# A two-layer decoder step: tables in the source fix the order of four engines' queues, and the first norm sums into two single banks

## The chip, the cores and the metric

The kernel runs on one core of a Trainium2 chip. The time is the device time of one execution in microseconds (us); three runs of the kernel before gave 983.78 (the median), 988.02 and 983.61 us.

In what follows, PE is the engine for matrix products (PEld its loading of the stationary operand), DVE the vector engine, ACT the engine for activation functions, POOL the general-purpose one, and SP the engine whose queue issues the transfers (DMAs). Each works through a queue of its own in order; an instruction that has to wait for another engine holds up what stands behind it in its queue.

## The reference

One step of a decoder trunk with two layers, for a prompt of 512 tokens and for 8 samples of 4 new tokens each, with D = 1024 and 16 heads of 64. Every layer computes, in float32,

```
x <- x + W_out( mixer(RMSNorm(x)) * silu(z) )        # z: a gate path out of the layer's input projection
layer 0: mixer = RWKV-7   # token shift, low-rank decay and gates, then per head
                          #   S_t = S_(t-1) (diag(w_t) - kk_t (a_t kk_t)^T) + v_t k_t^T ;  o_t = S_t r_t
layer 1: mixer = NSA      # 16 query heads, 4 KV heads, three branches that are gated and summed:
                          #   attention over compressed blocks (32 rows, stride 16),
                          #   over the 16 best blocks of 64 rows, and over a window of 512 rows
```

The results are the new x, the recurrence's states, the shift rows and the K/V rows of both groups.

## The kernel before

**Layout.** The 544 tokens stand as columns in two halves of 272 (256 of the prompt, 16 of the samples); features are on the partitions. Each float32 operand is split into a high and a low part (line L300 writes the high part on ACT, L301 the rest on POOL or DVE), and `products` (L339) takes three products for each block of 128 features: high x high, high x low, low x high. Such a matmul has the form 128*128 128x272; it goes to the sums `ph` or `pp` in PSUM. PE's stream is mostly these. They are also the filler around everything that waits.

**Layer 0.** First the norm (`rstd`: squares on ACT in pairs, `L418` sums them over the partitions with a matrix of ones, `L420` takes the logarithm, `L421` the exponential), then the projections, then the recurrence in chunks: a triangular inversion by 32 small steps (`L1139` multiply and `L1140` reduce, on DVE, for all heads at once, with tiles `tmp` and `i`), transposes (`L1167`), small products of 64x64 and 32x32 on PE (`L1171`, `L1180`, `L1190`, `L1333`, `L1340`, `L1354`, and from then on `L1237` to `L1292` chunk by chunk) with a mask or a sum on DVE behind each (`L1173`, `L1181`, `L1336`, `L1345`, `L1346`, `L1356`, `L1243`, `L1245`, `L1259`), and the samples' own recurrence (`L1311`, `L1378`, `L1379`, `L1385`, `L1394`, `L1397`, `L1402`). The gates' products run beside them as filler, and so does the first part of the output projection.

**Layer 1.** The input projection again by L339 into `ph`, scaled by the norm's row on DVE (`L1594`), the query and key norms (`L1601`, `L1608`, `L1610`, `L1613`); the attention for the prompt in blocks of 128 queries, `L1855` scores into `pq`, `L1882` bias, mask and row maximum (DVE), `L1889` the exponential (ACT), `L1894` to `L1909` the normalising (DVE, on ACT as `L1907`), `L1933` transposes of the weights into another `pq`, `L1936` (ACT) and `L1938` (DVE) copies of these out of PSUM, `L1946` and `L1949` products with the values into `pw`. The compressed branch has weights `cc`, transposed at `L1921`. The samples' attention (`L2007`, `L2014`, `L2029`, `L2050`, `L2084`) lies between; the gate products `L1643` to `L1656` stand at the start of the layer. The output projection is L339 and `L2127` with `L2141` adding the residual, and its last part `L2209` with `L2210`. The two `pq` tiles, one `pw` and three `ph` are all that layer 1 has in PSUM: whoever wants the next `pq` waits until one has been read.

**What sets the order.** The kernel is traced once in Python; the generators in it say which pieces follow each other, and then the library's scheduler sets the order of each engine's queue, by its own estimate of durations:

```
    with tile.TileContext(nc, schedule_with_timeline_sim=True) as tc, ExitStack() as ctx:
        build(nc, tc, ctx, I, O)
```

So the order in the queues isn't the one in the source, and no line of the source names it.

Of the kernel before, what the change touches and what calls it, by code (L numbers as in the profile page):

```python
# [228 lines left out]
class K:  # L229
# [175 lines left out]

    def rstd(self, X):
        nc = self.nc
        pt = self.PP()
# [1879 lines left out]
```

## Time and profile before

| | |
|---|---|
| times of three runs | 983.61, 983.78, 988.02 us |
| the profiled execution | 991.15 us, span 989.4 us, mean granted clock of PE 0.975 |
| busy | PE 937.0 us (95%), DVE 661.6 (67%), ACT 565.0 (57%), POOL 396.1 (40%) |
| the chain that ended last | PE 51%, DVE 14%, DMA 6%, ACT 5%, issue 5%, POOL 2% |
| transfers | 157.47 MB, 159 GB/s mean |

A profile is one execution; its rows show when each instruction started, for how long it ran, and what released it when its engine had been idle. The profiled execution took 7.4 us more than the median of the three runs (0.75%), so durations out of it are set against its own 991.15 us first.

A row of the timeline gives start and duration in us, engine, line, operation, the tile written and the tiles read, the form, how many instructions the row groups, and in brackets the engine's idle time ahead of it in us with its releaser. A row of the waits gives a waiting line, what it waited for, the total in us, how often, and the longest. A row of the table by stretches gives for each engine busy us and instructions, and after POOL the granted clock of PE (1.00 is full speed), the busy share of the transfer engines and GB/s.

### The profile page before, as it was taken

How to read it: one execution, taken by the hardware profiler on the slowest of the kernel's cores; microseconds unless marked ns; L12 is line 12 of the kernel's file. 1: busy time of each engine (PE TensorE's matmuls, PEld its weight loads, DVE VectorE, ACT ScalarE, POOL GpSimd, SP SyncE). 2: the span in 40 equal slices, each digit the busy share in tenths (PEclk: the TensorE clock that was granted, in tenths of full speed). 3: DMA queues.
4: the chain of work that ended last, by engine and by line, in shares of the span. 5: the costliest groups of instructions: out<-in, count | busy, mean ns of one | idle time of the engine just before them, and what ended most of it. 6: DMA issues, size and time to landing. Idle time of an engine off the chain costs nothing.

```text
span 989.4 us, 24773 instructions
## 1 busy us (share of the span) xinstructions
PE 937.0 (95%) x9445; PEld 843.5 (85%) x9445; DVE 661.6 (67%) x1533; ACT 565.0 (57%) x1369; POOL 396.1 (40%) x480
## 2 busy tenths in 40 slices
PE   8899999999799998999999999999898999999997
PEld 7889998889787787887888889998787898887987
DVE  6987778897847442456867734846877466748755
ACT  5455786565262345535645646756767675857542
POOL 4416645453320544230313576554344253341430
PEclk9999999999897997999989999999999999999999
DMA  5686236569383344564564596432634433476634
GB/s 193 183 268 210 65 118 204 166 197 281 104 231 92 124 141 139 162 200 101 168 194 129 190 280 226 142 99 75 161 95 121 118 99 124 116 188 211 199 117 136
DMA packets 149240, 157.47 MB, mean 159 GB/s; under 512 B 52226, under 2 KB 97058, under 8 KB 148866
## 3 DMA queue, kind: packets, MB, share of 16 engines
q1 hardware_dynamic: 149122, 155.90, 52.3%
q8 instruction: 74, 1.21, 0.5%
q14 instruction: 44, 0.36, 0.1%
HBM read 112.25 MB, written 43.80 MB: 158 GB/s over the span
## 4 chain that ended last, share of the span: by engine, by line
PE 51%; DVE 14%; DMA 6%; ACT 5%; issue 5%; POOL 2%; SPq 2%; DVEq 0%; POOLq 0%; ACTq 0%
PE ph L339 24%; PE pq L1855 3%; PE pw L1946 3%; PE pq L1933 3%; PE pr L1237 2%; DVE tmp L1139 1%; ACT l L300 1%; PE ph L2209 1%; PE ph L384 1%; POOL l L301 1%; PE s L1271 1%; DVE a L1909 1%; DMA d<-dram 1%; ACT a L1889 1%; DVE l L301 1%
## 5 line engine op out<-in xcount | busy, mean ns | idle before, releaser
L339 PE MATMUL ph<-x,l 128*128 128x272 f32 x2412 | 349.3, 296 | 4.5 <-DVE l L301 1.6
L339 PEld LDWEIGHTS ph<-x,l 128*128 128x128 f32 x2412 | 318.9, 192 | 18.9 <-issue 7.1
L301 POOL TENSOR_TENSOR l<-w,l 128x512 fp32r<-128x512 f32 (+2 forms) x118 | 157.0, 1341 | 157.6 <-ACT l L300 146.8
L300 ACT ACTIVATE l<-w 128x512 fp32r<-128x512 f32 (+2 forms) x152 | 88.9, 612 | 102.5 <-PE ph L339 47.9
L339 PE MATMUL pp<-x,l 128*128 128x272 f32 x768 | 107.1, 293 | 1.7 <-DVE bs L682 1.7
L339 PEld LDWEIGHTS pp<-x,l 128*128 128x128 f32 x768 | 100.0, 188 | 3.8 <-issue 2.6
L1889 ACT ACTIVATE a<-a,st 128x512 f32<-128x512 f32 (+3 forms) x128 | 70.6, 553 | 23.2 <-DVE st L1882 22.8
L1855 PE MATMUL pq<-p,z 128*128 128x512 f32 (+7 forms) x288 | 58.5, 328 | 6.8 <-DVE st L1882 4.2
L1882 DVE CUSTOM_DVE_ANT_0 a<-pq,tb 128x512 f32<-128x512 f32 (+3 forms) x128 | 56.7, 485 | 8.8 <-PE pq L1855 8.6
L1855 PEld LDWEIGHTS pq<-p,z 128*128 128x128 f32 x288 | 42.7, 189 | 12.7 <-issue 4.4
L339 PE MATMUL pp<-t,l 128*128 128x272 f32 x384 | 53.0, 291 | 0.0
L1909 DVE TENSOR_SCALAR a<-a,st 128x128 f32<-128x128 f32 (+3 forms) x112 | 50.7, 507 | 0.7
L339 PEld LDWEIGHTS pp<-t,l 128*128 128x128 f32 x384 | 49.9, 188 | 0.5
L1933 PE MATMUL pq<-cst,a 128*128 128x128 f32 x320 | 48.9, 275 | 1.0 <-DVE a L1909 0.9
L1594 DVE TENSOR_TENSOR d<-ph,RS 128x272 f32<-128x272 f32 x56 | 24.3, 437 | 32.7 <-PE ph L339 32.0
L1933 PEld LDWEIGHTS pq<-cst,a 128*128 128x128 f32 x320 | 37.1, 140 | 4.8 <-issue 2.2
L1946 PE MATMUL pw<-h,p 128*64 128x256 f32 x320 | 38.1, 384 | 2.2 <-DVE h L1938 1.5
L1936 ACT ACTIVATE h<-pq 128x512 f32<-128x512 f32 x52 | 30.2, 592 | 16.5 <-PE pq L1933 16.3
L301 POOL TENSOR_TENSOR d<-d,d 128x544 fp32r<-128x544 f32 (+2 forms) x19 | 25.5, 1344 | 32.5 <-ACT d L300 32.4
L301 DVE TENSOR_TENSOR l<-w,l 128x512 fp32r<-128x512 f32 x34 | 32.6, 967 | 8.8 <-ACT l L300 4.4
L1237 PE MATMUL pr<-ab,ab 64*64 64x128 f32 x256 | 33.6, 281 | 1.3 <-ACT q L1223 0.7
L1946 PEld LDWEIGHTS pw<-h,p 128*64 128x64 f32 x320 | 21.6, 136 | 14.7 <-DVE h L1938 2.3
(454 smaller groups left out, 1937.7 us busy)
## 6 DMA issues: line engine op xcount, KB each, us to landing
w<-in_rkvz SPq DMA_DIRECT2D x64, 256.0 KB, 4.3
d<-dram SPq DMA_DIRECT2D x60, 272.0 KB, 3.6
w<-in_win SPq DMA_DIRECT2D x56, 256.0 KB, 3.0
dram<-d SPq DMA_DIRECT2D x48, 272.0 KB, 2.8
ab<-dram SPq DMA_DIRECT2D x32, 256.0 KB, 4.1
p<-in_xT SPq DMA_DIRECT2D x16, 272.0 KB, 5.2
tb<-dram SPq DMA_DIRECT2D x16, 264.0 KB, 7.6
dram<-uar SPq DMA_DIRECT2D x8, 512.0 KB
```

What stands on the lines that cost most here:

```text
L300: nc.scalar.activation(hi, raw, AF.Copy)
L301: (eng or nc.gpsimd).tensor_tensor(lo, raw, hi.bitcast(F32), OP.subtract)
L339: nc.tensor.matmul((pt[h][:m, :HN] if split else pt[:m, h, :HN]), a[:, k, :m], b[:, h * HN:(h + 1) * HN], start=(k == 0 and n == 0), stop= ...
L1237: nc.tensor.matmul(pg[par][r, i], BK[r, i, par], AR[r, i].rearrange("p a b -> p (a b)"), start=True, stop=True)
L1594: self.nc.vector.tensor_tensor(o, p, r, OP.mult)
L1855: nc.tensor.matmul(p[:, par], QZ[k, b][x][:, par, m], kk[:, lo:hi], start=(x == 0), stop=(x == 1))
L1882: nc.vector.tensor_tensor_reduce(out=P[par][j], in0=p[:, par, :n], in1=TB[k][:, g, o:o + n], scale=-1.0, scalar=3.0e38, op0=OP.add, op1=OP ...
L1889: nc.scalar.activation(P[par][j], P[par][j], AF.Exp, scale=-1.0, bias=st[:, 0, g, j + 1:j + 2], accum_out=st[:, 1, g, j + 1:j + 2])
L1909: (nc.gpsimd if e == "p" else nc.vector).tensor_scalar(pj, pj, rr, None, op0=OP.mult)
L1933: nc.tensor.transpose(pt[:, g % 2, g // 2], PB[g][j][:, c * 128:c * 128 + 128], ident)
L1936: nc.scalar.activation(w, pt, AF.Copy)
L1946: nc.tensor.matmul(po[r], v, W[x][:, par], start=(x == ns - 1), stop=False, skip_group_check=True)
```

## The change

Two things. First, four lists of numbers for layer 0's recurrence (`TURNS`) and four for layer 1 (`TURNS1`), one each for PE, DVE, ACT and POOL. `mark` notes how many instructions an engine has been given at that point; `queue` cuts what it has been given since into groups, at the numbers of its list, puts the groups into the list's order, and binds each instruction to the one ahead of it, without a semaphore, so that the scheduler has to keep that order. SP has no list. Second, `rstd` sums into two tiles of one bank each (`s0`, `s1`, a bank for each half of the columns) instead of the two-bank `pp`, and so takes the logarithm in two instructions, one for each half. The next users of `s0` and `s1`, the low-rank rows' products at L448, now come behind these reads.

```
+TURNS = {
+    "PE": [48, 0, 24, 19, 28, 22, 36, 64, 82, 73, ...
...
+TURNS1 = {
+    "PE": [0, 16, 41, 11, 27, 43, 13, 29, 45, 15, ...
...
     def rstd(self, X):
-        pt = self.PP()
+        pt = [self.t(tag, (128, 512)) for tag in ("s0", "s1")]
...
-        self.keep_busy(pt[:, 0, 0:128], 16, made, ones, ones)
+        self.keep_busy(pt[0][:, 0:128], 16, made, ones, ones)
...
-                self.squared = nc.tensor.matmul(pt[:, h, :HN], ones, ...
+                self.squared = nc.tensor.matmul(pt[h][:, :HN], ones, ...
...
-        nc.scalar.activation(self.h2(rs), pt[:, :, :HN], AF.Ln, bias=self.C("eps"))
+        for h in range(2):
+            nc.scalar.activation(self.h2(rs)[:, h], pt[h][:, :HN], AF.Ln, bias=self.C("eps"))
...
+        self.mark()
         sample = self.sample_wkv(arS, bkS, sgS, vS, ysb)
...
         for _ in project_out(1, (4, 8) if PLAN["WS"] else (0, 8)):
             pass
+        self.queue(TURNS)
+    def queue(self, turns):
+        for name, order in turns.items():
+            engine, first = self.marks[name]
+            traced = [i for i in self.nc.cur_bb.bb.instructions if i.engine == engine][first:]
+            spans = sorted(order)
+            ends = dict(zip(spans, spans[1:] + [len(traced)]))
+            line = [i for s in order for i in traced[s:ends[s]]]
+            for a, b in zip(line, line[1:]):
+                self.tc.add_manual_dep(b, a.name, ...NoSync..., reason="queue")
...
+    k.mark()
     k.cmp_weights(lambda shape: k.t("s", shape))
     k.dense_keys()
     k.layer1()
+    k.queue(TURNS1)
```

The queues that come of it are close to those before. Counted over instructions that both have: on PE 6926 of 7083 stand in the same order relative to each other, on DVE 1485 of 1535, on ACT 1204 of 1222, on POOL 478 of 485, among SP's transfers 868 of 889. The rest are some 25 local moves on PE, some 45 short ones on DVE and a few on the others. No product is added or taken away; ACT has one instruction more. Three places follow. In the changed source a line of the recurrence or later has a number 32 higher, and a tile's number is 1 or 2 higher.

DVE in the inversion at 253 us: the rows of `i1` are the inversion's steps, `L1167` the transpose that the products `L1171` wait for. Before:

```order
L1139 TENSOR_TENSOR tmp1_592_3426<-i1_591_3423 128x18
L1167 STREAM_TRANSPOSE q0_605_3488<-q0_604_3482 128x512
L1140 TENSOR_REDUCE i1_591_3423<-tmp1_592_3426 128x2x3
L1139 TENSOR_TENSOR tmp1_592_3426<-i1_591_3423 128x32
L1140 TENSOR_REDUCE i1_591_3423<-tmp1_592_3426 128x2x4
L1139 TENSOR_TENSOR tmp1_592_3426<-i1_591_3423 128x50
L1140 TENSOR_REDUCE i1_591_3423<-tmp1_592_3426 128x2x5
L1139 TENSOR_TENSOR tmp1_592_3426<-i1_591_3423 128x72
L1140 TENSOR_REDUCE i1_591_3423<-tmp1_592_3426 128x2x6
L1139 TENSOR_TENSOR tmp1_592_3426<-i1_591_3423 128x98
```

Changed:

```order
L1171 TENSOR_TENSOR tmp1_593_3428<-i1_592_3425 128x18
L1172 TENSOR_REDUCE i1_592_3425<-tmp1_593_3428 128x2x3
L1171 TENSOR_TENSOR tmp1_593_3428<-i1_592_3425 128x32
L1172 TENSOR_REDUCE i1_592_3425<-tmp1_593_3428 128x2x4
L1171 TENSOR_TENSOR tmp1_593_3428<-i1_592_3425 128x50
L1172 TENSOR_REDUCE i1_592_3425<-tmp1_593_3428 128x2x5
L1171 TENSOR_TENSOR tmp1_593_3428<-i1_592_3425 128x72
L1172 TENSOR_REDUCE i1_592_3425<-tmp1_593_3428 128x2x6
L1171 TENSOR_TENSOR tmp1_593_3428<-i1_592_3425 128x98
L1199 STREAM_TRANSPOSE q0_606_3490<-q0_605_3484 128x512
```

The transpose moved behind eight instructions of the inversion.

DVE at 302 to 306 us: `p` and `ph` belong to the samples' recurrence, `q0` is what PE's product L1253 of the prompt's chunk reads. Before:

```order
L1379 TENSOR_REDUCE p_648_3987<-p_680_4136 128x64
L1378 TENSOR_TENSOR p_686_4153<-ph_687_4155,cst_63 128x512
L1378 TENSOR_TENSOR p_684_4150<-ph_685_4152,cst_63 128x512
L1379 TENSOR_REDUCE p_648_3987<-p_686_4153 128x64
L1379 TENSOR_REDUCE p_648_3987<-p_684_4150 128x64
L1243 TENSOR_TENSOR q0_671_4082<-pr_669_4064,cst_63 64x4x64
L1245 TENSOR_TENSOR q0_671_4082<-pr_669_4064,cst_63 128x4x64
L1259 COPY f0_673_4096<-s0_672_4087 128x256
```

Changed:

```order
L1411 TENSOR_REDUCE p_649_3989<-p_681_4138 128x64
L1410 TENSOR_TENSOR p_687_4155<-ph_688_4157,cst_63 128x512
L1410 TENSOR_TENSOR p_685_4152<-ph_686_4154,cst_63 128x512
L1411 TENSOR_REDUCE p_649_3989<-p_687_4155 128x64
L1275 TENSOR_TENSOR q0_672_4084<-pr_670_4066,cst_63 64x4x64
L1411 TENSOR_REDUCE p_649_3989<-p_685_4152 128x64
L1277 TENSOR_TENSOR q0_672_4084<-pr_670_4066,cst_63 128x4x64
L1291 COPY f0_674_4098<-s0_673_4089 128x256
```

The mask L1243 of the second chunk (L1275 in the changed source) moved ahead of the last reduction L1379 (L1411). On PE, at the same place, four L1229, three L339 and twelve L1394 moved ahead of the L1253 that reads its result.

PE at 971 to 973 us, in the last block of queries: `pw` and `pq` take transposes of the attention weights `cc` and `a`, `ph` is the output projection's last part. Before:

```order
L2209 MATMUL ph_2260_13518<-x_2071_12388,l_2248_13467 128x272
L2209 MATMUL ph_2260_13518<-x_2072_12389,l_2248_13467 128x272
L2209 MATMUL ph_2260_13518<-x_2071_12388,l_2249_13468 128x272
L1921 MATMUL pw_2233_13402<-cst_63,cc_2203_13178 128x128
L1933 MATMUL pq_2235_13406<-cst_63,a_2221_13293 128x128
L1933 MATMUL pq_2239_13424<-cst_63,a_2221_13293 128x128
L1933 MATMUL pq_2235_13406<-cst_63,a_2222_13294 128x128
L1933 MATMUL pq_2239_13424<-cst_63,a_2222_13294 128x128
L2209 MATMUL ph_2262_13536<-x_2068_12384,l_2248_13467 128x272
```

Changed:

```order
L1953 MATMUL pw_2234_13404<-cst_63,cc_2204_13180 128x128
L1965 MATMUL pq_2236_13408<-cst_63,a_2222_13295 128x128
L1965 MATMUL pq_2240_13426<-cst_63,a_2222_13295 128x128
L1965 MATMUL pq_2236_13408<-cst_63,a_2223_13296 128x128
L1965 MATMUL pq_2240_13426<-cst_63,a_2223_13296 128x128
L2241 MATMUL ph_2261_13520<-x_2069_12386,l_2249_13469 128x272
L2241 MATMUL ph_2261_13520<-x_2070_12387,l_2249_13469 128x272
L2241 MATMUL ph_2261_13520<-x_2069_12386,l_2250_13470 128x272
```

The five transposes moved ahead of the six products of `ph_2260_13518`.

More of the change, by code (lines that the diff above doesn't have):

```diff
@@ L74 @@
     'Q1': 7,
+}
+TURNS = {
+    "PE": [48, 0, 24, 19, 28, 22, 36, 64, 82, 73, 95, 79, 114, 180, 143, 228, 192, 234, 164, 247, 326, 342, 327, 196, 336, 344, 408, 212, 262, 294, 278, 298, 416, 376, 310, 360, 378, 433, 466, 434, 392, 439, 477, 520, 450, 488, 529, 884, 492, 889, 496, 498, 500, 502, 504, 506, 508, 510, 538, 497, 499, 501, 503, 505, 507, 509, 511, 564, 547, 568, 614, 582, 513, 634, 594, 556, 595, 639, 890, 598, 620, 599, 625, 600, 627, 601, 628, 650, 708, 746, 684, 761, 685, 764, 916, 692, 917, 688, 918, 689, 920, 794, 694, 716, 786, 730, 789, 796, 820, 822, 824, 826, 828, 830, 832, 834, 922, 732, 766, 812, 778, 798, 806, 817, 821, 823, 825, 827, 829, 831, 804, 833, 835, 852, 850, 862, 900, 923, 1164, 948, 1179, 1188, 1238, 1214, 932, 1218, 1241, 1314, 964, 1266, 996, 1028, 980, 1029, 1264, 1318, 1012, 1044, 1320, 1328, 1108, 1092, 1115, 1326, 1333, 1124, 1336, 1338, 1340, 1342, 1337, 1339, 1341, 1343, 1346, 1348, 1350, 1345, 1347, 1349, 1351, 1144, 1150, 1152, 1154, 1156, 1158, 1160, 1162, 1352, 1382, 1149, 1151, 1153, 1155, 1157, 1159, 1161, 1163, 1180, 1230, 1390, 1181, 1234, 1282, 1284, 1286, 1288, 1290, 1292, 1294, 1296, 1409, 1452, 1222, 1283, 1285, 1287, 1289, 1291, 1293, 1295, 1297, 1300, 1457, 1302, 1304, 1306, 1308, 1310, 1312, 1412, 1463, 1274, 1299, 1301, 1303, 1305, 1307, 1309, 1311, 1313, 1358, 1413, 1374, 1424, 1465, 1474, 1470, 1480, 1472, 1487, 1498, 1494, 1514, 1506, 1508, 1507, 1509, 1520, 1562, 1620, 1546, 1548, 1550, 1547, 1549, 1551, 1621, 1588, 1643, 1670, 1604, 1681, 1698, 1655, 1702, 1730, 1732, 1734, 1736, 1738, 1740, 1742, 1744, 1707, 1714, 1690, 1719, 1731, 1733, 1735, 1737, 1739, 1741, 1743, 1745, 1748, 1750, 1752, 1754, 1756, 1758, 1760, 1708, 1710, 1722, 1711, 1727, 1798, 1747, 1749, 1751, 1753, 1755, 1757, 1709, 1759, 1761, 1712, 1775, 1801, 1778, 1713, 1781, 1809, 1796, 1838, 1797, 1846, 1878, 1880, 1882, 1884, 1886, 1888, 1890, 1892, 1870, 1879, 1881, 1883, 1885, 1887, 1889, 1891, 1893, 1942, 1894, 1896, 1898, 1900, 1902, 1904, 1906, 1908, 1943, 1895, 1897, 1899, 1901, 1903, 1905, 1907, 1909, 1954, 1910, 1974, 1926, 1998, 2006, 1990, 1959, 1994, 2000, 2002, 2022, 2024, 2026, 2028, 2001, 2030, 2032, 2034, 2036, 1982, 2023, 2025, 2027, 2029, 2031, 2033, 2035, 2004, 2037, 2086, 2038, 2040, 2042, 2044, 2046, 2048, 2050, 2052, 2005, 2014, 2087, 2015, 2039, 2041, 2043, 2045, 2047, 2049, 2051, 2053, 2099, 2122, 2246, 2054, 2123, 2145, 2102, 2070, 2103, 2146, 2247, 2110, 2125, 2141, 2248, 2180, 2252, 2181, 2253, 2267, 2164, 2166, 2168, 2170, 2172, 2174, 2176, 2178, 2133, 2165, 2167, 2169, 2171, 2173, 2175, 2177, 2179, 2186, 2270, 2148, 2187, 2221, 2243, 2156, 2244, 2271, 2306, 2227, 2189, 2276, 2263, 2228, 2290, 2292, 2277, 2294, 2296, 2298, 2300, 2302, 2278, 2304, 2291, 2293, 2295, 2297, 2299, 2301, 2255, 2279, 2303, 2305, 2321, 2282, 2330, 2280, 2312, 2337, 2281, 2349, 2385, 2402, 2377, 2404, 2433, 2425, 2394, 2436, 2447, 2426, 2445, 2450],
+    "DVE": [10, 15, 14, 17, 6, 0, 7, 5, 8, 21, 31, 38, 43, 58, 18, 59, 19, 65, 79, 20, 80, 23, 82, 24, 26, 25, 27, 83, 28, 84, 30, 85, 33, 86, 29, 51, 98, 52, 40, 35, 128, 42, 49, 47, 68, 66, 72, 67, 73, 53, 55, 70, 76, 74, 77, 54, 75, 56, 114, 78, 87, 94, 96, 95, 97, 129, 91, 130, 100, 116, 108, 118, 113, 122, 124, 112, 117, 120, 119, 123, 125, 148, 126, 131, 135, 144, 133, 146, 151, 147, 134, 149, 136, 157, 137, 152, 138, 168, 139, 142, 141, 143, 145, 160, 162, 150, 161, 163, 166, 172, 190, 159, 165, 174, 167, 170, 175, 171, 173, 176, 284, 178, 180, 179, 181, 184, 285, 183, 185, 188, 191, 187, 189, 331, 192, 332, 193, 195, 211, 213, 201, 194, 207, 212, 214, 208, 215, 217, 209, 216, 218, 196, 202, 229, 203, 230, 205, 231, 220, 234, 225, 221, 237, 239, 226, 235, 238, 240, 236, 241, 243, 245, 249, 247, 242, 244, 255, 261, 246, 265, 267, 248, 250, 275, 277, 252, 279, 266, 268, 251, 253, 281, 276, 269, 271, 278, 280, 288, 290, 263, 292, 302, 256, 303, 270, 264, 272, 307, 311, 289, 291, 259, 293, 257, 308, 316, 258, 260, 306, 314, 320, 323, 325, 328, 309, 313, 318, 322, 315, 274, 317, 286, 324, 327, 310, 319, 287, 294, 298, 300, 330, 297, 352, 351, 299, 368, 301, 329, 339, 347, 349, 334, 333, 335, 345, 348, 350, 346, 354, 356, 359, 355, 358, 366, 340, 367, 374, 341, 375, 360, 362, 365, 370, 373, 388, 361, 364, 387, 391, 371, 392, 372, 376, 390, 383, 394, 386, 395, 382, 385, 393, 397, 396, 399, 398, 401, 400, 403, 402, 405, 404, 407, 406, 409, 408, 411, 410, 413, 412, 414, 418, 415, 419, 423, 417, 421, 420, 424, 428, 422, 426, 429, 425, 431, 427, 430, 432],
+    "ACT": [10, 0, 8, 2, 17, 7, 18, 12, 28, 13, 23, 51, 24, 19, 26, 46, 38, 21, 30, 69, 47, 36, 49, 42, 50, 44, 53, 64, 57, 59, 62, 60, 63, 80, 65, 58, 68, 73, 72, 82, 71, 93, 76, 123, 77, 87, 124, 86, 88, 147, 94, 148, 117, 129, 118, 125, 130, 134, 131, 96, 132, 135, 133, 136, 102, 139, 110, 143, 116, 127, 159, 128, 126, 176, 160, 149, 246, 166, 164, 168, 170, 167, 169, 171, 180, 178, 276, 179, 181, 189, 187, 183, 185, 188, 184, 190, 194, 191, 186, 195, 201, 192, 199, 197, 200, 202, 206, 204, 214, 216, 215, 205, 217, 224, 220, 219, 225, 229, 226, 222, 230, 227, 221, 240, 232, 243, 251, 234, 255, 260, 235, 265, 268, 236, 250, 271, 259, 262, 267, 239, 270, 248, 289, 263, 301, 275, 302, 264, 280, 283, 279, 281, 284, 288, 278, 285, 291, 286, 305, 300, 316, 296, 303, 319, 307, 320, 308, 315, 309, 322, 311, 318, 312, 325, 321, 326, 324, 327, 336, 339, 334, 342, 337, 345, 340, 348, 343, 351, 346, 354, 349, 347, 352, 350, 353, 355],
+    "POOL": [6, 4, 2, 0, 3, 1, 10, 8, 5, 20, 39, 13, 11, 7, 15, 12, 18, 16, 40, 21, 23, 25, 22, 27, 24, 36, 29, 26, 28, 31, 30, 33, 32, 37, 43, 34, 44, 35, 38, 41, 54, 42, 45, 49, 48, 50, 63, 56, 59, 58, 60, 64, 83, 78, 80, 84, 82, 79, 86, 85, 87, 91, 89, 92, 95, 93, 97, 102, 100, 105, 103, 108, 106, 109],
+}
@@ L417, in rstd @@
             for h in range(2):
-                self.squared = nc.tensor.matmul(pt[:, h, :HN], ones, sq[0][:, h * HN:(h + 1) * HN], start=(k == 0), stop=(k == KT - 2))
+                self.squared = nc.tensor.matmul(pt[h][:, :HN], ones, sq[0][:, h * HN:(h + 1) * HN], start=(k == 0), stop=(k == KT - 2))
         rs = self.t("d")
-        nc.scalar.activation(self.h2(rs), pt[:, :, :HN], AF.Ln, bias=self.C("eps"))
+        for h in range(2):
+            nc.scalar.activation(self.h2(rs)[:, h], pt[h][:, :HN], AF.Ln, bias=self.C("eps"))
         nc.scalar.activation(rs, rs, AF.Exp, scale=-0.5)
@@ L998, in layer0, with mark @@
             pass
+        self.queue(TURNS)
[7 more added lines that the diff above has]
+            for a, b in zip(line, line[1:]):
+                self.tc.add_manual_dep(b, a.name, mybir.DependencyInfo(mybir.DependencyClass.NoSync, mybir.DependencyReason.DATA), reason="queue")
+    def mark(self):
+        nc, now = self.nc, self.nc.cur_bb.bb.instructions
+        self.marks = {n: (e.engine, sum(i.engine == e.engine for i in now)) for n, e in
+                      (("PE", nc.tensor), ("DVE", nc.vector), ("ACT", nc.scalar), ("POOL", nc.gpsimd), ("SP", nc.sync))}
     def row_scale(self):
```

4 lines of the change are left out of this document (added).

## The prediction

> **What bounds the kernel now.** I read the page first (busy time by engine, the granted clock), then the waits of PE, then the timeline of PE and of the releasing engine at each wait near which the change moves something, and the table by stretches for the clock.
>
> ```profile
> PE 937.0 (95%) x9445; PEld 843.5 (85%) x9445; DVE 661.6 (67%) x1533; ACT 565.0 (57%) x1369; POOL 396.1 (40%) x480
> PEclk9999999999897997999989999999999999999999
> ```
>
> PE is busy for 95% of the span, no other engine for more than 67%. A changed order neither adds nor removes a product, so it can gain only what PE idles, about 989 - 937 = 52 us with start and end, and what PE loses where its clock is low (the 7, 7, 8 and 8 in the second line; there the busy figure hides the loss). The waits near which something moves:
>
> ```profile
> PE pq L1855 <- DVE st L1882: 4.2, 3, 2.4
> PE ph L1354 <- DVE v L1346: 3.7, 1, 3.7
> PE pq L1855 <- DVE h L1938: 1.7, 1, 1.7
> PE pw L1946 <- DVE h L1938: 1.5, 1, 1.5
> PE s L1253 <- DVE q L1243: 1.2, 1, 1.2
> PE ph L1608 <- DVE s L2014: 1.0, 1, 1.0
> PE ph L339 <- DVE d L2141: 0.9, 1, 0.9
> PE pw L1946 <- ACT h L1936: 0.7, 1, 0.7
> PE pr L1286 <- ACT p L1292: 0.5, 1, 0.5
> PE ph L777 <- ACT p L1292: 0.5, 1, 0.5
> ```
>
> Each ends when another engine's queue reaches one instruction. So I ask at each place whether that instruction moves forward, whether PE's filler is ahead of it, and what ends next.
>
> **The change part by part.** *The norm.* One more ACT instruction at 13 us and the low-rank products behind both halves; nothing shows the halves' price, PE has products of other rows to run meanwhile. I take 0, from -0.3 to +0.3.
>
> *The inversion, 253 to 272 us.*
>
> ```profile
> 253.61 0.71 DVE L1167 STREAM_TRANSPOSE q<-q 128x512 f32<-128x512 f32 x1 [0.34 <-DMA q<-dram]
> 258.77 1.50 DVE L1139 TENSOR_TENSOR tmp<-i 128x162 f32<-128x162 f32 x1
> 260.65 0.50 DVE L1139 TENSOR_TENSOR tmp<-i 128x200 f32<-128x200 f32 x1
> 254.37 1.15 PE L1171 MATMUL pr<-q,p 64*64 64x64 f32 x32 [0.31 <-DVE i L1140]
> 261.81 1.22 PE L1180 MATMUL pr<-q,q 64*64 64x64 f32 x32 [1.34 <-DVE q L1173]
> 266.68 1.42 PE L1354 MATMUL ph<-v,v 32*32 32x32 f32 x32 [3.66 <-DVE v L1346]
> 262.00:267.00 5.00, 1.30 (x34) 1.06 (x32) 4.81 (x11) 0.00 (x0) 0.00 (x0) 0.76 0.19 30
> 267.00:270.00 3.00, 2.96 (x51) 2.64 (x53) 2.95 (x5) 0.00 (x0) 0.00 (x0) 0.50 0.02 5
> ```
>
> DVE bounds this stretch (4.81 of 5 us). The transpose no longer waits 0.34 us for its transfer, since eight inversion steps now run in that time; that comes off DVE's chain for sure. On PE, L1171 now comes ahead of nine L339 and L1180 ahead of eighteen: PE pauses earlier, for some 3.3 us ahead of L1171, and only about 1 us ahead of L1354. The steps also slide past other work: the step of 162 columns took 1.50 us, the next, larger one 0.50, so up to 1.0 may go there, or come. Behind the pause of 3.66 us PE ran at half clock (0.50); if that goes, half of the last row's 3 us more at most. Between 0.3 and 2.8 I take 1.2: the 0.34 whole, and of the rest, 1.0 and 1.5, a third, since the two need not come together.
>
> *The samples' reductions, 302 to 307 us.*
>
> ```profile
> 304.03 1.95 DVE L1379 TENSOR_REDUCE p<-p 128x64 f32<-128x512 f32 x2
> 306.01 0.43 DVE L1243 TENSOR_TENSOR q<-pr,cst 64x256 f32<-64x256 f32 x1
> 306.49 0.67 PE L1253 MATMUL s<-q,q 64*64 64x64 f32 x14 [1.24 <-DVE q L1243]
> 305.50:309.00 3.50, 2.51 (x33) 1.86 (x35) 2.44 (x6) 1.86 (x5) 0.00 (x0) 0.99 0.02 5
> 309.00:326.00 17.00, 17.00 (x176) 14.15 (x174) 7.35 (x16) 2.89 (x7) 2.84 (x3) 0.50 0.35 94
> 320.92 4.45 PE L339 MATMUL ph<-x,l 128*128 128x272 f32 x18
> 577.82 3.67 PE L339 MATMUL ph<-x,l 128*128 128x272 f32 x28
> 585.60:588.80 3.20, 3.20 (x16) 3.20 (x16) 0.71 (x3) 1.53 (x3) 1.29 (x1) 0.50 1.13 282
> ```
>
> L1243 now comes ahead of the second L1379 (half of 1.95 us), and PE has three L339 and twelve L1394 to run until then; the 1.24 us go but for a remainder: 1.1. The table by stretches shows more: for 17 us behind this pause the clock is 0.50. Eighteen L339 take 4.45 us there (247 ns each), 28 at full clock 3.67 (131 ns). At full clock the 17 us would shrink by at most half, 8.5. What drops the clock isn't in the rows; the drop follows a stretch with PE busy for 2.51 of 3.50 us, mostly in small products, and the change fills 1.1 of that. The shortest stretch at half clock in this trace is the last row's 3.2 us; the 17 are about five times that. So the stretch may stay, lose one or more fifths at half of 3.2 = 1.6 us each, go, or a new short one may come. Between -1.6 and 8.5 I take 2.0, nearest to one fifth less. [...]
>
> *The recurrence's later chunks, 500 to 585 us.* The two waits for L1292 (0.5 each): ACT takes L1292 ahead of one or two L300, PE the filler behind. 0.8 together with a wait of 0.3 at 573, less what the passed L300 cost; from -0.5 to 1.2. At 583 PE also waits, for POOL:
>
> ```profile
> 583.26 1.26 POOL L301 TENSOR_TENSOR l<-w,l 128x512 fp32r<-128x512 f32 x1
> ```
>
> L1645 moves ahead of two POOL instructions, but the L339 behind need the tile that this L301 ends at 584.52, as before: 0.
>
> *Layer 1.*
>
> ```profile
> 695.59 0.74 DVE L1613 SCALAR_TENSOR_TENSOR p<-d,qkn,d 128x512 f32<-128x512 f32 x1
> 696.42 0.68 DVE L1938 COPY h<-pq 128x512 f32<-128x512 f32 x1
> 708.92 1.54 DVE L1909 TENSOR_SCALAR a<-a,st 128x384 f32<-128x384 f32 x4
> 743.88 0.22 DVE L1894 TENSOR_REDUCE st<-cc 128x2 f32<-128x64 f32 x1
> 851.80 2.14 DVE L1909 TENSOR_SCALAR a<-a,st 128x512 f32<-128x512 f32 x2
> 853.86 0.68 DVE L1938 COPY h<-pq 128x512 f32<-128x512 f32 x1
> 851.18 0.65 ACT L396 ACTIVATE d<-d 128x544 f32<-128x544 f32 x1
> 908.11 0.87 DVE L1692 TENSOR_TENSOR z<-q,z 64x256 fp32r<-64x256 f32 x2
> 909.23 0.43 DVE L2141 TENSOR_TENSOR d<-ph,d 128x272 f32<-128x272 f32 x1
> 974.30 1.04 PE L1933 MATMUL pq<-cst,a 128*128 128x128 f32 x8
> 975.43 0.60 ACT L1936 ACTIVATE h<-pq 128x512 f32<-128x512 f32 x1 [1.48 <-PE pq L1933]
> ```
>
> At 685 (the 2.4 of the 4.2) L1594 moves ahead of one L1882: PE restarts with other products at the same time: 0. At 697 the copy L1938 passes two L1613 (696.42 - 695.59 = 0.83), and L1594, which PE needs next, ends 0.1 later: 0.55, from 0 to 0.8. At 711 L2014 passes four L1909 (1.54), so the 1.0 goes down to what its own products leave; the copy behind the L1909 comes 0.8 later, with 2 us to spare: 0.8, from 0 to 0.95. At 744 the 0.22 of L1894 now stands ahead of the L1882 that PE waits for: -0.25, from -0.5 to 0. At 854 L1938 passes both L1909 (2.14), but ACT puts the 0.65 of L396 ahead of its L1936, which delays the transposes: of 1.46 I take 0.95, from 0.5. At 910 L2141 passes two L1692 (0.87) and small L301, and starts some 1.2 us earlier, behind L1938; that ends the 0.9. Ahead of it, at 904, PE's wait for L1936 goes, but the next `pq` is then free only when DVE, without a gap there, has read the last one: -0.3. So 0.5, from -0.3 to 1.5. At 976 five transposes go ahead of six L2209 (0.75), so ACT's L1936 no longer idles 1.48 us and the 0.7 ahead of L1946 goes with a part of what precedes: 0.95, from 0.5 to 1.0. The transfers that SP's queue moves (21 of 889) are loads and stores that end no wait of PE at these places, and POOL's moves pass only the mask sums at 583; both 0.
>
> The sum: 1.2 + 1.1 + 2.0 + 0.8 + 0.55 + 0.8 - 0.25 + 0.95 + 0.5 + 0.95 = 8.6 us. Off the profiled execution's 991.15 that leaves 982.55, a ratio of 0.9913; of the median 983.78, which lies 0.75% below the profiled execution, 975.2.
>
> **The rivals.** (1) *The clock stays as it is*: the pauses go, the 17 us stay at half clock. 8.6 - 2.0 = 6.6: 977.2. [...] (2) *The stretch at half clock goes whole*, 7 of the 8.5 us, since small products still wait for each other: 6.6 + 7 = 13.6, 970.3. (3) *The pauses only move*, as at 583 and 685: DVE's queue, full at 262 (4.81 of 5 us), hands out the same results at the same rate, and half of the 6.6 is all that is kept: 980.5, no change that can be told. (4) *Slower*: the pause ahead of L1171, 0.31 us now and some 3.3 then, is about as long as the 3.66 which half clock follows, and only small products stand behind it. If they hold the clock at 0.50 as long as behind 309, it costs up to 8.5 us; it decides if no L339 run within the next few us. With (3) that is 5.2 slower, 989.0; with all gains kept about 985.7. That the change does nothing is out: the queues of the built kernel stand in the tables' order.
>
> **How the numbers follow.** The forecast (5 to 11 us gained) has 0.35, (1) 0.20, (2) 0.17, (3) 0.20, (4) 0.08. A measurement of this kernel can tell about 0.5%, 4.9 us, from no change. Faster by more: the forecast, (1) and (2), less 0.04 for ends of the forecast and (1) that fall short, 0.68; within: (3), that 0.04 and a little of (4), 0.25; slower 0.07. The range leaves out (4), the poorer half of (3)'s spread and the far end of (2): 967.5 to 982.0; the clock's bounds make it that wide.
>
> **What would show it.** PE's waits for L1243, L2014, L2141 and L1938 at 306, 711, 910, 697 and 854 gone or below 0.3; that for L1936 at 976 gone; those at 583 and 685 still there; a longer pause ahead of L1171 and about 1 us ahead of L1354. In the clock's row, what follows 305. It is wrong if PE waits as much as before at other lines, or if half clock appears where it was full.

## The result, and the profile after

The changed kernel takes 974.41 us (median of 8 runs, 970.32 to 977.64), the kernel before, run beside it, 981.92 (median of 8, 978.77 to 988.02). The ratio is 0.9914, 95% interval 0.9885 to 0.9942; the forecast was 0.9913. Run again in the second experiment, it gave 0.9952 (0.9922 to 0.9981). Over all its 20 runs and 82 later runs of before, the means are 975.0 and 982.4 us: 7.4 us, standard error 0.9. So the forecast of 8.6 was right in direction and a little high; that the first ratio meets it to 0.0001 is luck, and its terms have to be looked at one by one. The ratios leave out runs more than 1.5% above the fastest of their kernel (4 of 12 for the recurrence's table alone, 3 of 12 for its early part), so the differences of the means over all runs are given beside them. The profiled execution of after took 970.95 us (span 969.2), 3.5 us less than its median, that of before 9.2 us more than 981.92. The 20 us between the two profiles must therefore not be read as the gain.

The page of after, busy time and granted clock:

```profile
PE 927.8 (96%) x9445; PEld 834.6 (86%) x9445; DVE 659.5 (68%) x1533; ACT 565.7 (58%) x1370; POOL 397.7 (41%) x480
PEclk9899999999999999999999989999999999999999
```

Before had 8, 7, 7 and 8 as low digits; here are two 8, the second at the same work as before's last (around L1646, here L1678). PE is idle 969.2 - 927.8 = 41.4 us, before 52.4. The lines in this kernel are 32 higher than before from the recurrence on (L1167 is now L1199, L1243 is L1275, L1292 is L1324, L1354 is L1386, L1938 is L1970), and the helpers L300, L301 and L339 are L312, L313 and L351. PE's waits (total, number, longest):

```profile
PE pr L1203 <- DVE q L1199: 4.2, 2, 3.6
PE ph L351 <- DVE d L1626: 2.1, 1, 2.1
PE pw L1675 <- ACT d L410: 1.6, 1, 1.6
PE pq L1887 <- DVE h L1970: 1.6, 2, 0.9
PE pq L1965 <- DVE a L1941: 1.3, 2, 1.1
PE pw L1978 <- ACT h L1968: 0.9, 1, 0.9
PE pr L1318 <- ACT p L1324: 0.5, 1, 0.5
PE ph L790 <- ACT p L1324: 0.5, 1, 0.5
```

The waits of before for L2014 and L2141, that of L1354 for L1346 and that of L1946 for L1938 have no row any more. That for L1243 (now L1275) at the samples' reductions is gone too; a row of 0.4 us that names it belongs to a later chunk, at 469 us. New are 3.6 us ahead of L1203 (before L1171), and 0.9 ahead of L1978. The two for L1324 (before L1292) stand as they were. PE's and DVE's timeline at the inversion and the samples' reductions:

```profile
252.51 0.70 DVE L1199 STREAM_TRANSPOSE q<-q 128x512 f32<-128x512 f32 x1
254.64 1.11 DVE L1171 TENSOR_TENSOR tmp<-i 128x162 f32<-128x162 f32 x1
256.14 1.42 DVE L1171 TENSOR_TENSOR tmp<-i 128x200 f32<-128x200 f32 x1
...
253.26 1.22 PE L1203 MATMUL pr<-q,p 64*64 64x64 f32 x26 [3.59 <-DVE q L1199]
263.67 0.38 PE L1386 MATMUL ph<-v,v 32*32 32x32 f32 x12
...
300.39 0.43 DVE L1275 TENSOR_TENSOR q<-pr,cst 64x256 f32<-64x256 f32 x1
300.85 1.03 DVE L1411 TENSOR_REDUCE p<-p 128x64 f32<-128x512 f32 x1
302.04 0.62 PE L1285 MATMUL s<-q,q 64*64 64x64 f32 x13
```

The transpose starts without its wait of 0.34. The step of 200 columns took 0.50 us in before and 1.42 here; the rows don't say why. L1386 has no pause ahead of it (before 3.66 us), L1275 now starts ahead of the reduction, and L1285 no longer waits. The table by stretches of after (PE, PEld, DVE, ACT, POOL busy, then granted clock, DMA share, GB/s):

```profile
249.60:253.20 3.60, 0.07 (x1) 0.00 (x0) 3.19 (x15) 1.14 (x3) 1.12 (x3) 1.00 0.47 151
253.20:257.80 4.60, 4.54 (x70) 4.17 (x70) 4.43 (x8) 2.32 (x5) 4.45 (x5) 0.63 0.40 126
263.67:296.42 32.75, 32.70 (x633) 26.98 (x634) 20.94 (x33) 16.38 (x39) 5.24 (x4) 1.00 0.61 177
304.00:321.00 17.00, 17.00 (x251) 13.35 (x248) 11.27 (x26) 4.77 (x12) 7.37 (x8) 1.00 0.48 142
```

Half clock now follows the pause at 250 (clock 0.63 over 4.6 us, that is 0.50 for 3.4). The part from the first L1386 to the first L1285 runs at full clock in 32.75 us; in before it was

```profile
266.68:301.23 34.55, 34.41 (x625) 28.50 (x627) 21.67 (x34) 16.39 (x39) 5.22 (x4) 0.93 0.59 168
```

with its first 4.7 us at 0.50. Nothing stands at half clock behind the reductions.

**A sum that fits every profile.** Each span can be split into PE's idle time, what half clock adds (estimated as half of PE's busy time in stretches at 0.50; in before an L339 took 247 ns in such a stretch and 131 at full clock), and the rest, PE's work at full clock. For before 52.4 + 22.6 + 914.4 = 989.4, for after 41.4 + 10.1 + 917.7 = 969.2. The rest is 914 to 918 us in all ten profiles of this document that have no products added, so idle time and clock make up the account to within 4 us.

### The profile page after: what moved, and what is told of

It reads as the page before. It is cut to its first block, busy times and chain, and to the rows that moved or that the text cites. A ratio compares the mean times of both kernels' runs of the same rounds, so it can differ in the third digit from the quotient of the medians.

```text
span 969.2 us, 24764 instructions
## 1 busy us (share of the span) xinstructions
PE 927.8 (96%) x9445; PEld 834.6 (86%) x9445; DVE 659.5 (68%) x1533; ACT 565.7 (58%) x1370; POOL 397.7 (41%) x480
## 4 chain that ended last, share of the span: by engine, by line
PE 70%; DVE 10%; DMA 7%; ACT 5%; issue 3%; SPq 3%; POOL 2%; DVEq 0%; POOLq 0%; ACTq 0%
PE ph L351 26%; PE pp L351 12%; PE pq L1887 4%; PE pq L1965 3%; PE pw L1978 3%; DMA d<-dram 2%; PE pr L1269 1%; PE ph L2241 1%; PE s L1593 1%; POOL l L313 1%; DVE tmp L1171 1%; PE pr L1321 1%; DVE a L1941 1%; PE s L1285 1%; PE s L1303 1%
## 5 line engine op out<-in xcount | busy, mean ns | idle before, releaser
L351 PE MATMUL ph<-x,l 128*128 128x272 f32 x2412 | 348.3, 295 | 4.3 <-DVE d L1626 2.1
L351 PEld LDWEIGHTS ph<-x,l 128*128 128x128 f32 x2412 | 316.1, 190 | 19.6 <-issue 6.9
L313 POOL TENSOR_TENSOR l<-w,l 128x512 fp32r<-128x512 f32 (+2 forms) x118 | 158.2, 1353 | 151.2 <-ACT l L312 133.8
L312 ACT ACTIVATE l<-w 128x512 fp32r<-128x512 f32 (+2 forms) x152 | 88.6, 611 | 86.0 <-PE ph L351 32.5
L351 PE MATMUL pp<-x,l 128*128 128x272 f32 x768 | 107.1, 293 | 1.7 <-DVE bs L695 1.7
L351 PEld LDWEIGHTS pp<-x,l 128*128 128x128 f32 x768 | 100.0, 188 | 3.8 <-issue 2.6
L351 PE MATMUL pp<-t,l 128*128 128x272 f32 x384 | 53.0, 291 | 0.0
L351 PEld LDWEIGHTS pp<-t,l 128*128 128x128 f32 x384 | 49.9, 188 | 0.5
L1978 PE MATMUL pw<-h,p 128*64 128x256 f32 x320 | 38.1, 384 | 0.9 <-ACT h L1968 0.9
L313 POOL TENSOR_TENSOR d<-d,d 128x544 fp32r<-128x544 f32 (+2 forms) x19 | 25.1, 1323 | 31.3 <-ACT d L312 31.2
L313 DVE TENSOR_TENSOR l<-w,l 128x512 fp32r<-128x512 f32 x34 | 31.1, 921 | 7.8 <-DMA dram<-l 4.2
L1934 POOL TENSOR_TENSOR cc<-cc,st 128x64 f32<-128x64 f32 x32 | 11.8, 368 | 53.3 <-DVE st L1931 37.6
```

Source lines behind the costliest of these rows:

```text
L312: nc.scalar.activation(hi, raw, AF.Copy)
L313: (eng or nc.gpsimd).tensor_tensor(lo, raw, hi.bitcast(F32), OP.subtract)
L351: nc.tensor.matmul((pt[h][:m, :HN] if split else pt[:m, h, :HN]), a[:, k, :m], b[:, h * HN:(h + 1) * HN], start=(k == 0 and n == 0), stop= ...
L1978: nc.tensor.matmul(po[r], v, W[x][:, par], start=(x == ns - 1), stop=False, skip_group_check=True)
```

## The experiments

Times are compared with runs of before on the same chip; "mean" is the difference of the means of all runs with its standard error.

**1. The three parts of the change, each alone.** Each kernel is the changed one with one or two of these taken back:

```
 e1_norm:        - k.queue(TURNS1)      - self.queue(TURNS)
 e1_recurrence:  - k.queue(TURNS1)      rstd as before
 e1_layer1:      - self.queue(TURNS)    rstd as before
 e1_both_tables:                        rstd as before
```

> The norm's part alone (its sums in the two single banks, one more ACT instruction); the order of the queues behind it is left as before. By the prediction: no change, 981.9 within 0.3 us. Rival, from PE's idle time ahead of 240 us (about 12.4 us before, about 8.9 after the whole change, four pauses at 56, 66, 149 and 186 us shorter): if the norm brings that, 3.5 us faster, 978.4. The two profiles each show one execution, so this may also be how DVE's steps happened to fall in one of them; then those pauses differ here too and the time does not.

> The recurrence's table alone; norm and layer 1 as before. By the prediction's terms: 1.2 + 1.1 + 2.0 (clock) + 0.8 = 5.1 us faster, 976.8. By PE's idle time between 240 and 600 us in the two profiles (21.0 us before, 17.0 after): 4.0 faster, 977.9, and the clock nothing. Rival 'it is all the clock': the long half-clock stretch behind 305 us goes and the gain is 7 or more, 975 or less. Rival 'the pauses only move': the new pause of 3.6 us ahead of L1171 eats them, 1 us or less, 981.

> Layer 1's table alone; norm and recurrence as before. By the prediction's terms: 0.55 + 0.8 - 0.25 + 0.95 + 0.5 + 0.95 = 3.5 us faster, 978.4. By PE's idle time behind 600 us (15.4 before, 11.8 after): 3.6, the same. Rival 'the pauses only move': 1 us or less. Rival 'it is all the clock': none, 981.9, since all but a tenth of the half-clock time lies ahead of layer 1; the stretches of before (309 to 326 among them) should then be seen here unchanged.

> Both tables, the norm as before. By the prediction: the whole 8.6, 973.3, as the changed kernel. Rival of the norm: 3.5 us less gain than the changed kernel, about 977.9. If the parts simply add, this is the sum of the two tables alone; if one table's gain depends on the other's state of the clock, it is not.

PE's idle time is counted from 240 to 600 us of the profile (the recurrence) and from 600 us to its end (layer 1):

| kernel | ratio, 95% interval | mean, us | idle in the recurrence, in layer 1, us |
|---|---|---|---|
| norm alone | 0.9997 (0.9962 to 1.0033) | -0.3 ± 1.4 | 21.7, 18.2 |
| recurrence's table | 0.9938 (0.9898 to 0.9979) | -2.2 ± 1.9 | 17.0, 18.4 |
| layer 1's table | 0.9963 (0.9928 to 0.9997) | -4.0 ± 1.2 | 20.6, 16.1 |
| both tables | 0.9896 (0.9852 to 0.994) | -9.4 ± 1.3 | 17.5, 14.7 |
| (before; after) | | | 20.8, 19.0; 17.1, 15.5 |

For the recurrence's table the mean is the safer figure, since its fastest run, 967.30, lies 9 us below the next. The three parts add up to some 6.5 us by their means (standard error about 2.6), against 7.4 for the whole, so they add within the noise. The idle time answers each table where it stands and nowhere else: 20.6 to 21.7 us without the recurrence's table, 17.0 to 17.5 with it; 18.2 to 19.0 without layer 1's, 14.7 to 16.1 with it. The norm alone shows no gain (-0.3 ± 1.4), and its rival of 3.5 us falls: the pauses at 56, 149 and 186 us differ between executions of one order (ahead of the first L1171 PE idles 12.5 us in before and 8.5 with layer 1's table alone, which leaves that part as it was). "All the clock" falls too, since layer 1's table gains 4.0 at an unchanged mean clock (0.9848; before, run beside it, 0.9849).

The kernel with the norm alone has the recurrence's old order. Its row at the stretch on which the clock term rested:

```profile
305.20:309.50 4.30, 3.41 (x48) 2.45 (x47) 3.24 (x6) 2.94 (x7) 0.00 (x0) 1.00 0.26 59
309.50:326.50 17.00, 17.00 (x263) 13.05 (x264) 10.62 (x26) 5.38 (x13) 6.17 (x7) 1.00 0.45 125
```

Nearly the same pause (0.9 us in L1253, PE idle for 0.9 of the first 4.3 us), and full clock behind it. The 17 us at half clock are in one profile, and in no other of the same order.

**2. Pauses filled with idle products; two copies moved back.** Added in the first and the third kernel, `fill` placing products ones times ones ahead of the real one on PE's queue, and in the fourth two entries of layer 1's table for ACT:

```
+ self.fill(pm[:, 0:128], 28)   # e2_fill_before: ahead of L1354; 10 more ahead of L1253
+ self.fill(pm[:, 0:128], 24)   # e2_fill_after: ahead of the second L1203; 11 and 13 later
 e2_copies, "ACT":
- 362, 403, 389, 369, 391        - 387, 415, 407, 416, 388, 392
+ 362, 369, 403, 389, 391        + 387, 388, 415, 407, 416, 392
```

> The order of before (with the changed norm), and in two of its pauses idle products whose result nothing reads (ones times ones into a PSUM tile that the next real product overwrites): 28 of 128 columns in the pause of 3.66 us ahead of L1354, 10 in the pause of 1.24 us ahead of L1253. DVE's and ACT's orders are untouched. If half clock behind these pauses is what the recurrence's table removed: the half-clock stretch at 264 (two windows of 3.4 us in all three profiles with this order, 2.0 to 3.0 us lost) goes, the part from the first L1354 to the first L1253 shortens from 34.5 to 35.1 us to about 32.7 as with the table, no stretch stands behind 306, and the time falls by 2 to 5 us, to 977 to 980. If the gain came from the order of DVE's steps alone: that part stays at 34.5, the time at 981.8.

> The changed kernel once more, beside the others. The prediction's 8.6 us: 973.2. By the pauses alone (PE's idle time 4.0 less in the recurrence, 3.3 less in layer 1, in three profiles each): 7.3, 974.5. By mean clocks of the runs so far (0.9849 before, 0.9856 after, times 980 us) the clock adds 0.7.

> The changed kernel with idle products in three of the pauses that half clock follows: 24 ahead of the second L1203 (the inversion's, 3.59 us), 11 ahead of L1222 at 364 us (1.38), 13 ahead of L1675 at 563 us (1.58). If PE's low activity in a pause is what halves the clock: the stretches at 254, 367 and 565 us (1.7 + 1.7 + 3.4 us lost in the changed kernel's profile) go, the mean clock rises from 0.986 to 0.990 or more, and the time falls by 3 to 6 us, to 968 to 971. If half clock comes from something else (the mixture of small products, what other engines do): no change, 974, or up to 2 us slower where a pause was shorter than its idle products.

> The changed kernel, with two of ACT's copies L1968 in layer 1 back ahead of the L408 (before: L396) that its table put in front of them. By the term for 854 (0.65 of L396 ahead of L1936 'delays the transposes'): PE's wait of 0.85 us for L1968 ahead of L1978 at 825 us and that of 0.58 ahead of L1965 at 836 go, 1.4 us or 0.15%, less than can be timed: 973 to 974.4, read from the waits. Rival: DVE's copy L1970 or L1914 ends the same waits a little later, and they stay above half their length.

Measured, in this order: 1.0104 (1.0074 to 1.0133), 0.9952 (0.9922 to 0.9981), 1.005 (1.0022 to 1.0078) and 0.992 (0.9891 to 0.9949). Both fills came out some 10 us slower than the kernel that they were added to (990.76 against 981.08 us, 984.63 against 974.32) where 2 to 6 less were expected, because the expectations took a product for one matmul; each of these products stands in the trace as two, which take 0.115 us each. PE's timeline in the filled after, and one row of ACT's:

```profile
250.88 5.52 PE L1039 MATMUL pr<-ones 128*128 128x128 f32 x48
...
585.42 0.63 ACT L312 ACTIVATE l<-w 128x512 fp32r<-128x512 f32 x1 [7.00 <-DMA w<-in_win]
586.11 4.22 PE L351 MATMUL ph<-x,l 128*128 128x272 f32 x17 [4.77 <-ACT l L312]
```

24 products are 48 matmuls and 5.52 us, in a pause of 3.6; the 11 took 2.6 us at 356 us, where PE had no pause. In all 96 matmuls were added, 11 us. Three things can still be read. In the filled before, the part from the first L1354 to the first L1253 runs at full clock, as expected; it takes 35.13 us, but 2.5 of them are the second fill. In the filled after, from the first L1171 to the first L1354 nothing is lost to half clock, where the five profiles of the table's order so far, with the pause open, lose 1.7 to 3.4 us. And where the pause at 563 us was filled and the clock stayed up, PE then stood 4.77 us for its weights, which ACT could not prepare ahead of their transfer. The table by stretches there, same kernel:

```profile
572.00:578.00 6.00, 5.93 (x47) 5.69 (x46) 2.00 (x6) 2.10 (x5) 2.64 (x5) 1.00 1.07 260
578.00:584.00 6.00, 3.34 (x27) 3.12 (x25) 0.00 (x0) 0.43 (x1) 5.50 (x8) 1.00 1.04 233
```

The busy share of the DMA engines is 1.07 and 1.04 there. In after this stretch ran its first 6.8 us at half clock (564.54 to 571.37 us, PE busy throughout, share 1.08) and had no such wait, with PE busy for all of the 12 us from 575 to 587: half clock may have cost nothing there that the transfers didn't take anyway. This is one execution, so a reading and no proof.

The copies hold what was expected. Of after, ACT and PE around 825 and 836 us:

```profile
823.15 0.66 ACT L408 ACTIVATE d<-d 128x544 f32<-128x544 f32 x1 [3.60 <-DVE d L1626]
823.84 0.66 ACT L409 ACTIVATE d<-d 128x544 f32<-128x544 f32 x1
824.41 0.58 ACT L1968 ACTIVATE h<-pq 128x512 f32<-128x512 f32 x1
...
825.04 1.95 PE L1978 MATMUL pw<-h,p 128*64 128x256 f32 x16 [0.85 <-ACT h L1968]
...
832.78 1.20 PE L1887 MATMUL pq<-p,z 128*128 128x512 f32 x4 [0.49 <-DVE st L1914]
...
836.07 0.66 PE L1965 MATMUL pq<-cst,a 128*128 128x128 f32 x4 [0.58 <-ACT h L1968]
```

and the same products with the copies ahead of L408:

```profile
838.57 1.95 PE L1978 MATMUL pw<-h,p 128*64 128x256 f32 x16
...
848.37 0.60 PE L1965 MATMUL pq<-cst,a 128*128 128x128 f32 x4
849.07 1.20 PE L1887 MATMUL pq<-p,z 128*128 128x512 f32 x4
```

All three waits, 0.85, 0.49 and 0.58, are gone; layer 1's idle time is 14.0 us (after: 15.5, again 15.1). This version had the lower median beside after (973.86 against 974.32) and beats before; that it beats after, its 1 us of idle time says and the clocked times cannot.

**3. The recurrence's table cut in two, and the fill at its right size.** The cut is where the first chunk's L1253 ends; each half takes all instructions that this needs from one order and the rest from the other.

```
 e3_early:  TURNS  = after's order up to the cut, then before's     TURNS1 = before's order
 e3_late:   TURNS  = before's order up to the cut, then after's     TURNS1 = before's order
 e3_fill14: both in before's order, + self.fill(pm[:, 0:128], 14) ahead of L1354
```

> The changed norm; of the recurrence's table only the first part, all that stands ahead of the end of the first chunk's L1253 (the inversion and the samples' reductions); the rest of the recurrence and layer 1 in the order of before. By the prediction's terms: 1.2 + 1.1 + 2.0 (clock) = 4.3 us faster, 977.1 where before runs at 981.4. By the parts of the profiles so far (from the first L1171 to the first L1253 58.3 to 60.6 us in three profiles of the old order, 56.1 to 58.3 in five of the new; the pause of 0.9 to 1.2 us in L1253 gone): 3 to 4 us, with no stretch at 309. If the gain of the recurrence lay in the later chunks: 1 us or less.

> The opposite: the inversion and the samples' reductions in the order of before, the rest of the recurrence in the table's; layer 1 as before. By the prediction: 0.8 us faster, 980.6. By PE's idle time in the profiles (from 330 us to the copy L777 6.4 to 6.7 us before, 6.2 to 8.7 after; from there to L1646 5.5 before, 4.8 after): nothing, 981.4, from 0.7 faster to 1 slower, and the waits for L1292 (0.48, 0.47 us) stand unchanged, against the prediction. The pauses of 3.65 us ahead of L1354 and of 0.9 to 1.2 in L1253 are back.

> The order of before, with 14 idle products (each passes PE twice, 0.23 us, so 3.2 us in all) in the pause of 3.66 us ahead of L1354 and nowhere else; the 28 of the earlier run took 6.4 us and held L1354 up. If the half clock behind this pause is what the old order loses: no half clock from the first L1354 to the first L1253, that part 32.7 us and not 34.5 to 35.1, as the table has it, and 2 us less in all, 979.4. If that part is bound by DVE, and PE's clock in it costs nothing: it stays at 34.5, at full clock, with more idle time, and the time at 981.4.

Measured: early 0.9932 (0.9896 to 0.9969), mean -5.0 ± 1.7; late 0.9982 (0.9951 to 1.0013), -1.8 ± 1.3; fill 1.0004 (0.9967 to 1.0041), +0.7 ± 1.8. The recurrence's gain lies mostly in its early part, as predicted (4.3): its idle time is 17.6 us in the early kernel and 19.8 in the late one, against 21.0 in the old order. In the late kernel the 3.65 us ahead of L1354 are back (263.9), and the waits for L1292 stand at 0.48 and 0.47. PE's timeline in the filled kernel:

```profile
270.99 3.39 PE L1042 MATMUL s<-ones 128*128 128x128 f32 x28 [0.27 <-DVE p L1237]
274.39 0.79 PE L1410 MATMUL ph<-v,v 32*32 32x32 f32 x17
```

and its table by stretches, from the first L1354 (here L1410) to the first L1253:

```profile
274.39:307.62 33.23, 32.62 (x625) 26.80 (x627) 21.52 (x34) 16.38 (x39) 5.21 (x4) 1.00 0.60 175
```

With the old order and the pause filled, the part behind L1354 runs at full clock and takes 33.23 us; with half clock it takes 34.55 to 35.27 (before, norm alone, layer 1's table, late), with the table's order 32.73 to 33.09 (six profiles). So what this part loses in the old order is mostly the half clock behind the pause. The total didn't fall by the expected 2 us. In this profile half clock stood ahead of the pause instead (262.3, for 3.4 us), and the part ahead of L1354 took 26.20, above the 23.64 to 26.00 of the old order. Whether filling the pause gains anything in all stays open.

## Why the prediction was right, and where not

**Right in sum.** PE's idle time fell by 3.8 us in the recurrence (means: 21.0 over three profiles of the old order, 17.3 over five of the new) and by 3.2 in layer 1 (18.6 over six, 15.3 over four); together 7.0, predicted 6.6. The clock gave less than its term. The sum came out by errors that cancel: the terms of 2.0 and 0.8 gave less, the inversion more. Where it went, term by term (pauses of before's profile against after's, or means over profiles):

| term | predicted | measured |
|---|---|---|
| inversion | 1.2 | 2.4: first L1171 to first L1253 59.6 us in four profiles of the old order, 57.2 in six of the new |
| samples' reductions | 1.1 | 1.0: waits of 1.2, 0.9, 1.2 in three profiles of the old order gone in six of six of the new |
| clock behind 305 | 2.0 | 0.8 ± 0.5 for the whole kernel |
| later chunks | 0.8 | 0.1: idle time up to L777 6.7 to 7.8, waits from there to the one at 583 3.7 to 2.5 |
| 583 | 0 | -0.2 |
| 685 | 0 | 0.35: 2.45 to 2.11 |
| 697 | 0.55 | 0.83: 1.73 to 0.90 |
| 711 | 0.8 | 0.95: gone |
| 744 | -0.25 | -0.34: 0.33 to 0.67 |
| 749 | not named | 0.7: 1.39 + 0.69 to 0.34 + 1.05 |
| 854 | 0.95 | -0.46: 1.46 to 0.85 + 0.49 + 0.58 |
| 904 to 910 | 0.5 | 0.8: 0.65 + 0.90 to 0.74 |
| 976 | 0.95 | 0.75: 0.75 + 0.73 to 0.73 |

Layer 1 sums to 3.6 against 3.5, with two terms that failed in opposite directions: 749 was not seen and 854 had the wrong sign. The rows above layer 1 don't add: the inversion's 2.4 are in part clock, which the third row counts for the whole kernel.

**The inversion was mis-sized,** within its range but too low. The pause ahead of L1171 came as predicted (3.59 in after), while that ahead of L1354 went whole and not down to about 1 us (in the kernel with the recurrence's table alone 0.8 stayed). I took a third of what the half clock behind 3.66 us of pause might give back. It was the larger piece: 2.0 to 3.0 us are lost from the first L1354 to the first L1253 in the four profiles of the old order with this pause open, 0 in six of six with the new one. Rival 4 had the danger right, a drop behind L1171, and its price wrong: the drop came (1.7 to 3.4 us of PE's time), but it falls where DVE bounds the stretch (4.43 of 4.60 us busy in the row at 253.20), and the part around it is no longer than before, 23.4 to 25.6 us against 23.6 to 26.0. Before and after, from the first L1171 to the first L1354:

```profile
242.93:266.68 23.75, 17.01 (x277) 16.21 (x277) 18.94 (x38) 7.48 (x14) 13.11 (x14) 0.96 0.58 159
239.82:263.67 23.85, 19.66 (x270) 17.78 (x269) 19.62 (x39) 7.90 (x15) 13.62 (x15) 0.93 0.55 157
```

PE idles 6.7 us in the first row and 4.2 in the second, and the part is as long. So most of the idle time that fell in the recurrence fell where it bought next to nothing: in the means over the four old and six new profiles 2.5 us of it went here, while half clock took 1.9 us more and the part shortened by 0.4 (24.7 to 24.4). The gain of the inversion is that half clock moved from behind L1354, where PE is busy throughout (32.70 of 32.75 us), to a part where PE has idle time.

**The clock term rested on one execution.** Of five profiles of the old order with its pauses open (before, norm alone, layer 1's table, late, and the filled kernel, whose pause at L1253 is open), one shows the 17 us at 0.50. (The row of 3.2 us, by which the term was measured, cuts at round times a stretch of 3.41.) Rival 1, "the clock stays as it is", is nearer than the forecast's 2.0: over all runs the mean granted clock is 0.9844 in 118 runs with the recurrence's old order and 0.9855 in 57 with the new one (difference 0.0011 ± 0.0007). In the 82 runs of before a clock higher by 0.01 goes with 6.9 us less, so this is worth 0.8 ± 0.5 us. A gain of 0 isn't excluded by this.

**The later chunks: the mechanism failed.** I read PE's two waits for L1292 as ACT's queue, held by L300. The timeline of before around the first of them:

```profile
502.79 0.38 ACT L1292 ACTIVATE p<-pr 128x256 f32<-128x256 f32 x1
...
502.05 0.69 PE L1289 MATMUL pr<-q,q 128*64 128x64 f32 x16
503.22 0.68 PE L1286 MATMUL pr<-ab,f 64*64 64x64 f32 x16 [0.48 <-ACT p L1292]
```

and the same in after:

```profile
485.26 0.38 ACT L1324 ACTIVATE p<-pr 128x256 f32<-128x256 f32 x1 [1.69 <-PE pr L1321]
...
484.53 0.69 PE L1321 MATMUL pr<-q,q 128*64 128x64 f32 x16
485.70 0.68 PE L1318 MATMUL pr<-ab,f 64*64 64x64 f32 x16 [0.48 <-ACT p L1324]
```

PE's product ends at 502.74, and ACT's copy starts 0.05 us later; nothing held it. The wait is the copy's own 0.38 and 0.1 around it. In after ACT stood ready for 1.69 us, and the wait is 0.48 as before. A releaser's name doesn't say that it was late: its start against its own input does. What the part behind L777 gained, 1.2, came at other waits, from 554 to 574 us in before, and the part ahead of it lost about as much (1.1).

**854 had the right parts and the wrong sum.** DVE's copy no longer holds L1946. I charged ACT's L396 (now L408) once, for its 0.65; the table puts it, with L409 behind it, ahead of two copies, at two places, and both became waits of PE (0.85 and 0.58). With these two moves taken back, neither wait is in the profile.

**Rivals.** "The pauses only move" would have kept half of the 6.6 us; idle time fell by 7.0 and the time by 7.4. "The stretch goes whole", 13.6 us, and "slower" did not come. Of the signs named beforehand, the waits for L1243, L2014 and L2141 and that of L1946 for L1938 are gone, 583 and 685 stand, 697 is not below 0.3 but 0.90, and 1 us ahead of L1354 was wrong. At 976 the wait for L1936 is gone. One sign of being wrong did appear, half clock where it had been full (at 253.9 us), without the price feared.

## What to carry to other kernels

Split each span into the busiest engine's work, its idle time and what its clock costs: here the first stayed within 4 us under every order, the second shows at the place which move worked, and the third must be read over many executions, because one profile's low-clock stretch need not be in the next (17 us at 0.50 behind 309 us in before, 17 us at 1.00 in the same place with the norm alone). Idle time and clock must then be read together, part by part: ahead of L1354 PE idled 2.5 us less here and lost 1.9 us more to half clock, and the part shortened by 0.4: half clock cost next to nothing there, where DVE bounds the stretch (4.43 of 4.60 us busy). That it is so where the transfers bound it (share 1.04 to 1.08), one execution suggests. Before a wait is put down to a queue, compare the releaser's start with the end of its own input; where they were 0.05 us apart, the new order didn't shorten it.

## What the runs showed of the hardware

In before, the stretches at half clock between 6 and 988 us start at 32.48, 264.59, 308.96, 380.64, 493.28 and 585.44 us and last 3.41, 6.83, 17.07, 10.24, 6.83 and 3.41 us. In after they start at 32.06, 45.72, 253.93, 366.57 and 564.54 us; the last is 6.83 us long, the others 3.41. All of these lengths, and the distances from one start to the next, are whole multiples of a fifth of the 17.07 us (3.41) to within 0.05 us; the 44.37 us from 264.59 to 308.96 are 13 of them.

Why the pause in L1253 was followed by half clock in before and not with layer 1's table alone stays open. In the 4.30 us ahead of the 17 us (304.66 to 308.96 us in before, 306.70 to 311.00 in the other) PE is busy for 3.06 us in both; the clock behind is 0.50 in the first and 1.00 in the second. PE's busy time just ahead of the other stretches doesn't settle it either. In the last 3.41 us ahead of each stretch at half clock, in the order above, it is 2.04, 1.22, 2.47, 1.47, 2.44 and 2.06 us in before, and 2.35, 3.14, 0.67, 1.57 and 1.83 in after. From 851.70 to 855.11 us in before it is 1.95, less than in several of these, and the clock stays at 1.00 behind it.

Nor does a long pause stand right ahead of each. In after, two rows of the table by stretches, cut where the clock falls at 45.72 us:

```profile
42.31:45.72 3.41, 3.14 (x28) 3.15 (x29) 3.41 (x8) 1.53 (x3) 0.69 (x2) 1.00 0.58 182
45.72:49.13 3.41, 3.41 (x19) 3.41 (x18) 3.41 (x6) 1.08 (x3) 0.00 (x0) 0.50 0.67 249
```

and, from PE's timeline, products in the first:

```profile
42.58 1.95 PE L1539 MATMUL s<-ca,cw 128*128 128x2 f32 x16 [1.26 <-ACT cb L1543]
```

PE counts as busy for 92% of the first row (3.14 of 3.41 us; it idles 0.27), 1.95 us of it with products of two columns, and the clock is 0.50 behind it. The spread between runs of one kernel (974.56 to 994.21 us for before) goes with the clock: the correlation of time and mean granted clock is -0.82 over 82 runs.
